# Two heads' scores issued in turn, a padded up-projection and a new order of head groups in a two-layer hybrid attention trunk

## The chip, the cores and the metric

The kernel runs on one core of a Trainium2 chip. The metric is the time of one execution on the device, in microseconds (us); of several runs the median counts. TensorE appears in the views as PE (matmuls) and PEld (loads of the stationary operand), VectorE as DVE, ScalarE as ACT, GpSimd as POOL, SyncE, whose queue issues the transfers, as SP.

## The reference, cut to what matters

Two layers over 512 tokens of width 1024. In each, one projection of the normed stream feeds five groups of four heads of width 64; their outputs go through one output projection, and a gated MLP of width 2816 with a short causal convolution follows.

```python
q_a = _heads(_rms_norm(cq, ...) @ mla_w_uq[l], 4)       # latent rank 192 -> 4 x 96
kv_a = _heads(_rms_norm(ckv, ...) @ mla_w_ukv[l], 4)    # latent rank 128
o_a = _dense_causal_attention(q_a, k_a, v_a, 96 ** -0.5)               # "mla"
o_b = _dense_causal_attention(q_b, k_b, v_b, 64 ** -0.5, decay)        # "fox"
o_c = _moba_attention(q_c, k_c, v_c, 64 ** -0.5)                       # "moba"
o_d = _diff_causal_attention(q1, q2, k1, k2, v_d, lam, 32 ** -0.5)     # "diff"
o_e = _memory_attention(q_e, k_e, v_e, 64 ** -0.5)                     # "mem", 256 keys
x = x + concat(o_a, o_b, o_c, o_d, o_e) @ w_o[l]
x = x + (silu(conv(n @ w_gate)) * (n @ w_up)) @ w_down
```

With 512 tokens every past key is within moba's choice, so that fox and moba are causal over all keys, with 128, 256, 384 and 512 keys for the four blocks of 128 rows; mem always has 256.

## The kernel before, in words

Tokens come in four blocks of 128. The heads of a group are worked on in pairs. A pair's queries and keys of width 64 lie in one tile `qk_t`: head 0 in partitions 0 to 63, head 1 in 64 to 127. Every operand of a product is held as a high and a low part in float32r, and a product is three passes: high by high, high by low, low by high. A score block of fox, moba or mem is thus three matmuls that read 64 partitions (TensorE's records say `64*128`: 64 rows and 128 columns of the array in use). Mla's heads are 96 wide; diff's are stacked to 128 rows and need one pass.

`Pair.step` (line 687) is one head and one row block: it takes one PSUM bank of the tag `s` (there are two), issues the three passes through `passes` (line 471), and then VectorE reduces the row minimum out of the bank (`soft`, line 623) and frees it, ScalarE takes the exponential (628), the rows are scaled (636, 638), TensorE transposes them (`put_pt`, 645) and they are copied into `pt_t`. `Pair.close` (754) multiplies with the values (776; for mem 768): here the two heads take turns, and they stand in different columns of the array (`128*64`). Fox adds a decay bias that POOL makes from a tile `R` per head (703, 708).

The latent up-projection (`up_proj`, 1247) multiplies plain float32 tiles: 128 rows of the latent, then its last 64, then the keys' and values' part. A float32 matmul is two records in the trace, a float32r one is one.

The order on each engine is fixed when the program is built. The work is written as tasks that ask for a buffer or for a turn on an engine at an assumed duration (`mm`, `tr`, `vec`, ... at lines 59 to 100). `Flow.run` gives out the turns by these durations: of the operations that are ready, the one that can start first, and of those the one of the earliest task. The list `ORDER` (924) sets which task is earlier: `p.` projects a pair, `a.` attends, `w.` is a group's part of the output projection, `kv.` the memory's keys and values. The chip then runs each engine's list in that order, and each instruction waits for what it needs.

Of the kernel before, what the change touches and what calls it, by code (L numbers as in the profile page):

```python
# [9 lines left out]
F32 = mybir.dt.float32  # L10
# [8 lines left out]
D = 1024  # L19
# [13 lines left out]
# 500000 ** (-i / 16) in float32, i = 0..15: the rotary frequencies of the  # L33
# 32-wide rotation; those of the 16- and 8-wide ones are every 2nd and 4th.
# [6 lines left out]
# packed small vectors, one row per layer  # L41
# [24 lines left out]

def tr(n):
    return "T", 109.0 * n
# [40 lines left out]
class Ticket(Event):  # L109
    # a place in the line for a buffer that is handed out in the order of asking  # L110
# [10 lines left out]
class Flow:  # L121
    # ns from the end of an operation to where an engine can use what it made
    LAT = {"T": dict(T=0, V=196, A=197), "V": dict(T=202, V=127, A=128, P=155, D=130),
           "A": dict(T=217, V=142, A=127, P=170), "P": dict(T=149, V=60, A=60, P=88),
           "D": dict.fromkeys("TVAPD", 2000)}

    # the engines that are short of time count for more where there is a choice
# [40 lines left out]
    def grant(self, tag):  # L168
        # first the line, then the tasks that ask without a ticket, earliest first
# [21 lines left out]
    def step(self, k, val):  # L191
        # issues what the last request was for, and takes the next one
# [81 lines left out]
def trunk(ctx: ExitStack, tc: tile.TileContext, x_in, mem, pos, norms, sm, lam, cols, conv,  # L274
# [10 lines left out]
    SLOTS = {"ws": 2, "wh": 6, "wl": 6, "qk": 4, "pt": 3, "v": 5, "kt": 1, "sk": 1, "mx": 2, "e": 5, "R": 1,  # L285
             "hr": 3, "qn": 3, "sq": 2, "st": 24, "acc": 2, "s": 2, "tp": 2, "o": 2}
# [14 lines left out]
    # ScalarE's tables: the set with both exp and ln, but for the gates the finer ln  # L301
# [26 lines left out]
    jp = const.tile([128, 128], I32, name="jp")  # L328
    P.iota(jp, pattern=[[1, 128]], base=0, channel_multiplier=-1)
# [6 lines left out]
    # the causal mask of a row block is the end of this one. It is MoBA's too: of the two  # L336
    # blocks of 256 keys that 512 tokens have, its top 3 are both, so that it sees every past key
# [3 lines left out]
    upto = const.tile([128, 128], F32, name="upto")  # L341
    V.tensor_scalar(upto, jp, 0.0, None, op0=OP.is_ge)
# [47 lines left out]
    # a block of weights as a sum of two float32r parts  # L390
# [94 lines left out]
    # half of the columns of a row block, transposed, into columns c0.. of dh + dl  # L485
# [21 lines left out]
    # sums of squares of the halves of a row block, as they come  # L507
# [1227 lines left out]
```

## Time and profile before

| what | value |
|---|---|
| runs | 1491.82, 1474.21, 1487.29 us |
| median | 1487.29 us |
| profiled execution, its span (no other time of it is given) | 1487.5 us |
| TensorE matmul busy | 1424.1 us, 96% of the span |
| VectorE, ScalarE, GpSimd busy | 757.1, 668.6, 810.6 us |
| mean granted TensorE clock | 0.977 of full speed |

The span falls into four parts: attention of the first layer to about 414 us, its MLP to 768, attention of the second layer to about 1132, its MLP to the end. A busy time of TensorE overlaps with the next matmul's, since they are pipelined; how much of the path a matmul takes is read from the distance between the starts of two rows.

### The profile page before, as it was taken

The page shows a single profiled execution, that of the slowest core. Times are in us where ns is not written, and L with a number is a line of the kernel's source. Part 1 is how long each engine was busy: PE and PEld are TensorE (multiplying, and loading weights), DVE is VectorE, ACT ScalarE, POOL GpSimd, SP SyncE. Part 2 cuts the span into 40 slices and gives each one's busy share as a digit, 9 for nine tenths or more (in the row PEclk, how much of TensorE's full clock was granted, in tenths as well). Part 3 has the DMA queues.
Part 4 walks back from the last instruction along what each step waited for, and adds up shares of the span by engine and source line. Part 5 has one row for each costly group of instructions (what it writes and reads, how often), then busy time and mean ns, then how long its engine had stood idle before and what let it go on. Part 6 is the DMA issues. An engine that isn't in the chain of part 4 may idle for free.

```text
span 1487.5 us, 20886 instructions
## 1 busy us (share of the span) xinstructions
PE 1424.1 (96%) x7304; PEld 1186.3 (80%) x7304; DVE 757.1 (51%) x2001; ACT 668.6 (45%) x1454; POOL 810.6 (54%) x793
## 2 busy tenths in 40 slices
PE   6999889999899999999999999989999999999998
PEld 5878778867798888888879788787778888888887
DVE  7977778856822311332048776887665231023311
ACT  5646546645544322433245475566544332233321
POOL 5657758642765445544466667666335443454443
PEclk9989999989999999999999899999899999999999
DMA  5211232103333223332231101210023322333223
GB/s 170 56 42 43 95 91 64 51 31 101 97 117 116 75 85 107 117 96 78 85 114 44 54 29 51 82 54 30 29 85 98 100 87 72 113 117 96 79 77 113
DMA packets 53112, 120.56 MB, mean 81 GB/s; under 512 B 6544, under 2 KB 7696, under 8 KB 53008
## 3 DMA queue, kind: packets, MB, share of 16 engines
q1 hardware_dynamic: 53008, 119.24, 25.6%
q8 instruction: 58, 0.95, 0.3%
q14 instruction: 46, 0.38, 0.1%
HBM read 117.11 MB, written 2.10 MB: 80 GB/s over the span
## 4 chain that ended last, share of the span: by engine, by line
PE 81%; DVE 10%; POOL 4%; issue 3%; ACT 1%; DMA 1%; SPq 0%; DVEq 0%; POOLq 0%; ACTq 0%
PE acc_p L471 28%; PE s_p L471 13%; PE o_p L471 8%; PE tp_p L471 8%; PE s_p L1596 4%; PE acc_p L1596 4%; PE tp_p L1596 4%; PE o_p L1596 4%; PE tp_p L645 3%; PE o_p L776 2%; DVE e_t L725 1%; POOL wl_t L414 1%; POOL st_t L481 1%; DVE qn_t L860 1%; DVE e_t L623 1%
## 5 line engine op out<-in xcount | busy, mean ns | idle before, releaser
L414 POOL TENSOR_TENSOR wl_t<-ws_t,wh_t 128x768 fp32r<-128x768 f32 (+2 forms) x280 | 451.3, 1616 | 442.1 <-ACT wh_t L412 426.5
L412 ACT ACTIVATE wh_t<-ws_t 128x768 fp32r<-128x768 f32 (+3 forms) x322 | 240.1, 749 | 443.5 <-DMA ws_t<-in_w_down_dram 81.7
L471 PE MATMUL acc_p<-wh_t,xh 128*128 128x384 f32 (+2 forms) x512 | 185.2, 362 | 1.3 <-ACT hr_t L313 0.7
L471 PE MATMUL acc_p<-wh_t,xl 128*128 128x384 f32 (+2 forms) x512 | 169.8, 332 | 0.0
L471 PE MATMUL acc_p<-wl_t,xh 128*128 128x384 f32 (+2 forms) x512 | 169.7, 331 | 0.0
L481 POOL TENSOR_TENSOR st_t<-st_t,misc 128x4 f32<-128x4 f32 (+4 forms) x96 | 110.6, 1155 | 80.1 <-DVE st_t L479 63.3
L628 ACT ACTIVATE e_t<-e_t,st_t 128x128 f32<-128x128 f32 (+3 forms) x192 | 105.2, 549 | 48.2 <-DVE st_t L623 42.8
L471 PE MATMUL acc_p<-wh_t,mx_t 128*128 128x512 f32 x320 | 119.0, 423 | 3.4 <-DVE x L905 3.3
L471 PEld LDWEIGHTS acc_p<-wh_t,xh 128*128 128x128 f32 x512 | 98.6, 193 | 7.4 <-issue 1.9
L471 PEld LDWEIGHTS acc_p<-wl_t,xh 128*128 128x128 f32 x512 | 98.6, 193 | 0.8
L471 PEld LDWEIGHTS acc_p<-wh_t,xl 128*128 128x128 f32 x512 | 97.9, 191 | 0.0
L623 DVE CUSTOM_DVE_ANT_0 e_t<-s_p,mask 128x256 f32<-128x256 f32 (+3 forms) x160 | 74.3, 471 | 26.8 <-PE s_p L471 20.0
L645 PE MATMUL tp_p<-identr,e_t 128*128 128x128 f32 x384 | 69.4, 282 | 13.9 <-DVE e_t L725 9.6
L471 PEld LDWEIGHTS acc_p<-wh_t,mx_t 128*128 128x128 f32 x320 | 62.7, 196 | 20.9 <-DVE x L905 5.2
L1535 DVE SCALAR_TENSOR_TENSOR e_t<-acc_p,convt,e_t 128x511 f32<-128x511 f32 x22 | 16.5, 750 | 123.3 <-ACT e_t L1533 123.3
L1535 DVE SCALAR_TENSOR_TENSOR e_t<-tp_p,convt,e_t 128x511 f32<-128x511 f32 x22 | 16.5, 750 | 121.2 <-ACT e_t L1533 121.2
L313 ACT ACTIVATE pt_t<-tp_p 128x256 f32<-128x256 f32 (+3 forms) x125 | 54.4, 437 | 52.4 <-PE tp_p L645 51.0
L645 PEld LDWEIGHTS tp_p<-identr,e_t 128*128 128x128 f32 x384 | 47.7, 143 | 33.1 <-issue 14.6
L471 PE MATMUL acc_p<-xh,wh_t 128*128 128x512 f32 (+1 forms) x192 | 72.0, 375 | 0.0
L471 PE MATMUL acc_p<-xl,wh_t 128*128 128x512 f32 (+1 forms) x192 | 71.7, 374 | 0.1
L471 PE MATMUL s_p<-xh,wh_t 128*128 128x512 f32 (+1 forms) x192 | 71.6, 373 | 0.0
L471 PE MATMUL acc_p<-xh,wl_t 128*128 128x512 f32 (+1 forms) x192 | 71.5, 373 | 0.0
(275 smaller groups left out, 3561.2 us busy)
## 6 DMA issues: line engine op xcount, KB each, us to landing
ws_t<-in_gu_dram SPq DMA_DIRECT2D x116, 384.0 KB, 3.0
ws_t<-in_w_down_dram SPq DMA_DIRECT2D x88, 256.0 KB, 2.5
ws_t<-in_win_pair_dram SPq DMA_DIRECT2D x48, 384.0 KB, 3.1
ws_t<-in_w_o_dram SPq DMA_DIRECT2D x40, 256.0 KB, 2.6
pt_t<-in_norms_dram SPq DMA_DIRECT2D x12, 256.0 KB, 4.0
ws_t<-in_mkv_dram SPq DMA_DIRECT2D x8, 384.0 KB, 3.0
ws_t<-in_win_mla_dram SPq DMA_DIRECT2D x8, 356.0 KB, 3.0
x<-in_x_dram SPq DMA_DIRECT2D x8, 256.0 KB, 6.9
```

Of the source, the lines that this page charges most:

```text
L313: A.activation(out, in_, AF.Copy)
L412: A.activation(self.h[:, :n], stg[:, :n], AF.Copy)
L414: ENG[e].tensor_tensor(out=self.l[:, :n], in0=stg[:, :n], in1=f32(self.h[:, :n]), op=OP.subtract)
L471: T.matmul(dst, lt, rh, start=first and i == 0, stop=last and i == n - 1)
L481: P.tensor_tensor(r[:, :n], v[:, :n], mhalf[:, :n], op=OP.pow)
L623: V.tensor_tensor_reduce(out=e[:, :n], in0=sbank[:, :n], in1=bias, scale=-scale, scalar=BIG, op0=OP.add, op1=OP.min, accum_out=st[:, 0:1])
L628: A.activation(e[:, :n], e[:, :n], AF.Exp, bias=st[:, 0:1], scale=-1.0, accum_out=st[:, 1:2])
L645: T.transpose(tp[:, j * 128:(j + 1) * 128], e[:, j * 128:(j + 1) * 128], ident)
L725: V.scalar_tensor_tensor(e[:, :n], e2[:, :n], st[:, 8:9], e[:, :n], op0=OP.mult, op1=OP.add)
L776: T.matmul(ob[h, 128 * j:512], self.src.vt[:, j, h], mv, start=j == 0, stop=j == 3)
L1535: V.scalar_tensor_tensor(c[:, 1:], bg[:, :S - 1], convt[:, f, 1:2], c[:, 1:], op0=OP.mult, op1=OP.add)
L1596: T.matmul(dbs[t][h], lt, (w.h, w.l)[wi][:, :512], start=fi == 0 and lt is gh and wi == 0, stop=fi == HALF_F - 1 and lt is gl)
```

## The change

- In fox, moba and mem one task (`scores`) now issues the score passes of both heads of a pair, head 0 and head 1 in turn, into both `s` banks; two further tasks (`rows`) do the softmax of one head each. It asks for both banks, and for both `e` buffers, before it issues anything. Mla and diff keep `step`.
- The 64 last rows of the latent are padded with zeros to 128, and so are the weights; two memsets on POOL per layer are new.
- `mm` and `tr` assume other durations, `mm2` is new: they change the order that is written, and no instruction.
- `ORDER` takes the first fox pair ahead of the second mla pair, and other places of mem, moba and `w.`.
- There are two `R` buffers. To make room, the triangle `upto` is built anew in each layer (one iota on POOL, one comparison on VectorE), the convolution's weights of 88 columns are loaded after the attention and not at the start, and `st` has 19 buffers and not 24.

```diff
 def mm(n, passes=1):
-    return "T", passes * (2 + max(107.0, 0.417 * n))
+    return "T", passes * max(109.0, 13.0 + 0.4155 * n)
...
+def mm2(n, passes):
+    return "T", passes * max(109.0, 16.0 + 0.4155 * n) + 200.0
...
 def tr(n):
-    return "T", 109.0 * n
+    return "T", 109.0 * n - 70.0
...
-            for a in range(2):
-                tk = ticket("pt")
-                op = task(self.open(a, tk))
-                heads.append([task(self.step(a, i, op)) for i in range(NT)])
+            tks = [ticket("pt") for _ in range(2)]
+            ops = [task(self.open(a, tk)) for a, tk in enumerate(tks)]
+            if kind in ("mla", "diff"):
+                for a in range(2):
+                    heads[a] = [task(self.step(a, i, ops[a])) for i in range(NT)]
+            else:
+                self.sc = [None] * NT
+                for i in range(NT):
+                    both = task(self.scores(i, ops))
+                    for a in range(2):
+                        heads[a].append(task(self.rows(a, i, both)))
...
+        def scores(self, i, ops):
+            kind, p = self.kind, self.p
+            yield ops + self.src.steps[:i + 1]
+            n, mk, qc = self.place(i)
+            qk = self.src.qk
+            yield "e", 2
+            es = [sbt([128, 512], "e") for _ in range(2)]
...
+            yield "s", 2
+            sbs = [bank("s") for _ in range(2)]
...
+            yield mm2(n, 3)
+            for j in range(3):
+                for a in range(2):
+                    lt, rh = parts[a][j]
+                    T.matmul(sbs[a][:, :n], lt, rh, start=j == 0, stop=j == 2)
...
+            yield gps1(512)
+            P.memset(Lt.t[64:128, 2, :], 0.0)
...
+            yield gps1(384)
+            P.memset(Up.q[64:128, 384:768], 0.0)
...
-                                      (lat_t[0:64, 2, ts_], uqt[0:64, q1:q1 + 192])], True, True)
+                                      (lat_t[:, 2, ts_], uqt[:, q1:q1 + 192])], True, True)
...
-    ORDER = ["p.mla0", "a.mla0", "p.fox1", "p.mla1", "a.mla1", "a.fox1", "p.fox0", "a.fox0", "p.diff0",
-             "w.fox", "kv.own", "a.diff0", "w.mla", "p.diff1", "a.diff1", "p.mem", "p.moba0", "a.mem1",
-             "a.mem0", "p.moba1", "a.moba0", "a.moba1", "w.diff", "w.mem", "w.moba", "kv.next"]
+    ORDER = ["p.mla0", "a.mla0", "p.fox0", "a.fox0", "p.mla1", "a.mla1", "p.fox1", "a.fox1", "p.diff0", "w.mla",
+             "kv.own", "a.diff0", "w.fox", "p.diff1", "a.diff1", "p.mem", "a.mem0", "p.moba0",
+             "a.mem1", "p.moba1", "a.moba0", "w.diff", "a.moba1", "w.mem", "w.moba", "kv.next"]
```

First place: TensorE in mem's attention of the first layer, before. `s_p<-kt_t,qk_t` are score passes (three are one head and one block), `acc_p<-wh_t,xh` and the like are projection passes of moba, `tp_p` are transpositions: of the normed queries and keys (`qn_t`), of softmax rows (`e_t`).

```order
L471 MATMUL s_p<-kt_t,qk_t 128x256 x3
L471 MATMUL acc_p<-wh_t,xh 128x384
L471 MATMUL acc_p<-wl_t,xh 128x384
L471 MATMUL acc_p<-wh_t,xl 128x384
L1350 MATMUL tp_p<-identr,qn_t 128x128 x2
L645 MATMUL tp_p<-identr,e_t 128x128 x2
L471 MATMUL s_p<-kt_t,qk_t 128x256 x6
```

The same place now:

```order
L745 MATMUL s_p<-kt_t,qk_t 128x256 x6
L479 MATMUL acc_p<-wh_t,xh 128x384
L479 MATMUL acc_p<-wl_t,xh 128x384
L479 MATMUL acc_p<-wh_t,xl 128x384
L479 MATMUL acc_p<-wh_t,xh 128x384
L479 MATMUL acc_p<-wl_t,xh 128x384
L479 MATMUL acc_p<-wh_t,xl 128x384
L745 MATMUL s_p<-kt_t,qk_t 128x256 x6
```

Before, score passes stand in runs of three, or of six where two blocks of one head follow each other; now every run is six passes of two heads. In the whole program 66 runs become 48.

Second place: TensorE at the end of the first mla pair, first layer, before. `acc_p<-wh_t,xh` and the like are the fox projection, the eight transpositions of `e_t` are mla's last softmax rows, `o_p<-pt_t,v_t` is mla's product with the values, `acc_p<-wh_t,pt_t` the up-projection of the second pair.

```order
L471 MATMUL acc_p<-wh_t,xh 128x384
L471 MATMUL acc_p<-wl_t,xh 128x384
L471 MATMUL acc_p<-wh_t,xl 128x384
L1350 MATMUL tp_p<-identr,qn_t 128x128 x2
L645 MATMUL tp_p<-identr,e_t 128x128 x8
L1350 MATMUL tp_p<-identr,qn_t 128x128 x2
L776 MATMUL o_p<-pt_t,v_t 64x512 x2
L776 MATMUL o_p<-pt_t,v_t 64x384 x2
L776 MATMUL o_p<-pt_t,v_t 64x256 x2
L776 MATMUL o_p<-pt_t,v_t 64x128 x2
L1350 MATMUL tp_p<-identr,qn_t 128x128 x2
L471 MATMUL acc_p<-wh_t,pt_t 128x192 x2
```

The same place now, from mla's last score passes (`s_p<-qk_t` of 512 keys) on; `tp_p<-identr,misc` are the transpositions for fox's bias:

```order
L479 MATMUL s_p<-qk_t 128x512 x6
L1411 MATMUL tp_p<-identr,qn_t 128x128 x4
L653 MATMUL tp_p<-identr,e_t 128x128 x8
L825 MATMUL o_p<-pt_t,v_t 64x512 x2
L825 MATMUL o_p<-pt_t,v_t 64x384 x2
L825 MATMUL o_p<-pt_t,v_t 64x256 x2
L825 MATMUL o_p<-pt_t,v_t 64x128 x2
L697 MATMUL tp_p<-identr,misc 128x128 x8
L479 MATMUL acc_p<-wh_t,pt_t 128x192 x2
```

No fox projection pass stands any longer between the last mla scores and the product with the values (twelve did); all of them have moved ahead of these scores. After the product, the transposition of normed fox queries that stood there is gone, and the transpositions of fox's bias and the second up-projection follow at once.

## Rows read from the trace of the kernel before

**Rows 1.** The page, part 1: busy us (share of the span) xinstructions.
```profile
PE 1424.1 (96%) x7304; PEld 1186.3 (80%) x7304; DVE 757.1 (51%) x2001; ACT 668.6 (45%) x1454; POOL 810.6 (54%) x793
```
**Rows 2.** Stretches: length, busy PE, PEld, DVE, ACT, POOL, clock, DMA share, GB/s.
```profile
40.00:80.00 40.00, 35.19 (x207) 29.57 (x206) 38.49 (x147) 25.20 (x65) 28.55 (x37) 1.00 0.19 53
103.00:158.00 55.00, 54.86 (x331) 44.36 (x331) 44.12 (x145) 35.38 (x96) 37.82 (x58) 1.00 0.09 30
283.00:310.00 27.00, 27.00 (x156) 20.45 (x153) 19.00 (x76) 16.96 (x52) 11.87 (x18) 1.00 0.07 23
322.00:365.00 43.00, 43.00 (x190) 30.82 (x190) 25.84 (x91) 24.18 (x63) 12.54 (x13) 0.84 0.22 65
414.00:768.00 354.00, 354.00 (x1630) 295.92 (x1629) 84.44 (x103) 121.01 (x180) 175.22 (x114) 1.00 0.31 98
```
**Rows 3.** Nine stretches at clock 0.50 inside the two attention parts, summed.
```profile
sum 67.40, PE 66.72 PEld 49.25 DVE 39.79 ACT 25.42 POOL 29.16; mean PE 7.41 PEld 5.47 DVE 4.42 ACT 2.82 POOL 3.24
```
**Rows 4.** Timeline, PE: one head's fox scores of 512 keys. Start us, length, instruction.
```profile
108.23 0.27 PE L645 MATMUL tp_p<-identr,e_t 128*128 128x128 f32 x1
108.44 0.96 PE L471 MATMUL s_p<-qk_t 64*128 64x512 f32 x3
109.33 0.44 PE L471 MATMUL acc_p<-wh_t,xh 128*128 128x384 f32 x1
109.61 0.34 PE L471 MATMUL acc_p<-wl_t,xh 128*128 128x384 f32 x1
```
**Rows 5.** Timeline: runs of three passes over 128, 384 and 256 keys.
```profile
103.21 0.55 PE L471 MATMUL s_p<-qk_t 64*128 64x128 f32 x3
103.69 0.44 PE L471 MATMUL acc_p<-wh_t,xh 128*128 128x384 f32 x1
...
106.54 0.79 PE L471 MATMUL s_p<-qk_t 64*128 64x384 f32 x3
107.25 0.44 PE L471 MATMUL acc_p<-wh_t,xh 128*128 128x384 f32 x1
...
288.93 0.62 PE L471 MATMUL s_p<-kt_t,qk_t 64*128 64x256 f32 x3
...
289.48 0.44 PE L471 MATMUL acc_p<-wh_t,xh 128*128 128x384 f32 x1
...
289.58 0.42 DVE L623 CUSTOM_DVE_ANT_0 e_t<-s_p,mask 128x256 f32<-128x256 f32 x1 [1.34 <-PE s_p L471]
```
**Rows 6.** Timeline, PE: a run of six passes over 256 keys.
```profile
283.68 0.97 PE L471 MATMUL s_p<-kt_t,qk_t 64*128 64x256 f32 x6
284.58 0.44 PE L471 MATMUL acc_p<-wh_t,xh 128*128 128x384 f32 x1
```
**Rows 7.** Timeline, PE: the latent queries' up-projection.
```profile
39.10 1.01 PE L471 MATMUL acc_p<-wh_t,pt_t 128*128 128x192 f32 x4
...
39.26 0.84 PE L471 MATMUL acc_p<-wh_t,pt_t 128*128 128x192 f32 x3
40.04 0.33 PE L1098 MATMUL tp_p<-identr,qn_t 128*128 128x128 f32 x1
```
**Rows 8.** Chain of waits in order of time: start us, us, what.
```profile
281.44 2.30 PE o_p L776 x16
...
436.28 5.44 PE s_p L471 x24
```
**Rows 9.** Line 623, the reduction out of the score bank: ns min/median/max.
```profile
L623 DVE CUSTOM_DVE_ANT_0 e_t<-s_p,mask x160: 273/425/694, 57.7 to 1089.7; 128x256 f32<-128x256 f32 x64, 128x128 f32<-128x128 f32 x32, 128x384 f32<-128x384 f32 x32, 128x512 f32<-128x512 f32 x32
```
**Rows 10.** Timeline, PE, end of the first mla pair.
```profile
67.38 0.95 PE L471 MATMUL s_p<-qk_t 96*128 96x512 f32 x3
...
74.78 2.91 PE L776 MATMUL o_p<-pt_t,v_t 128*64 128x512 f32 x16
80.28 0.77 PE L1350 MATMUL tp_p<-identr,qn_t 128*128 128x128 f32 x2 [2.59 <-DVE qn_t L853]
```

More of the change, by code (lines that the diff above doesn't have):

```diff
@@ L683, in open, with place @@
                 yield act(512)
-                A.activation(self.R, tp, AF.Copy, scale=-1.0)
+                A.activation(R, tp, AF.Copy, scale=-1.0)
                 free("tp")
+        def place(self, i):
+            n = M if self.kind == "mem" else 128 * (i + 1)
+            mk = mask[:, 0:M] if self.kind == "mem" else mask[:, 384 - 128 * i:512]
+            return n, mk, slice(128 * i, 128 * i + 128)
+        def scores(self, i, ops):
[5 more added lines that the diff above has]
+            es = [sbt([128, 512], "e") for _ in range(2)]
+            mks = [mk, mk]
+            if kind == "fox":
+                csb = misc[:, 96:112]
+                for a, e in enumerate(es):
+                    hd = 2 * p + a
+                    yield gps1(n)
+                    P.tensor_scalar(e[:, :n], self.R[a][:, :n], 1.0, csb[:, 4 * i + hd:4 * i + hd + 1],
+                                    op0=OP.mult, op1=OP.add)
+                    if i == NT - 1:
+                        free("R")
+                    yield gps(128)
+                    P.tensor_tensor(e[:, n - 128:n], e[:, n - 128:n], mask[:, 384:], op=OP.add)
+                    mks[a] = e[:, :n]
+            yield "s", 2
+            sbs = [bank("s") for _ in range(2)]
+            parts = []
+            for a in range(2):
+                r = slice(64 * a, 64 * a + 64)
+                if kind == "mem":
+                    kt = self.extra.kt
+                    qh, ql, kh, kl = qk[0][r, p, 0, qc], qk[0][r, p, 1, qc], kt[r, p, 0, :], kt[r, p, 1, :]
+                else:
+                    tl = qk[0]
+                    qh, ql, kh, kl = tl[r, 0, 0, qc], tl[r, 0, 1, qc], tl[r, 1, 0, 0:n], tl[r, 1, 1, 0:n]
+                parts.append([(qh, kh), (qh, kl), (ql, kh)])
+            yield mm2(n, 3)
+            for j in range(3):
+                for a in range(2):
+                    lt, rh = parts[a][j]
+                    T.matmul(sbs[a][:, :n], lt, rh, start=j == 0, stop=j == 2)
+            self.sc[i] = es, mks, sbs
@@ new lines, in rows, with turn @@
+        def rows(self, a, i, both):
+            yield both
+            n = self.place(i)[0]
+            es, mks, sbs = self.sc[i]
+            e, mk, sb_ = es[a], mks[a], sbs[a]
+            yield "st"
+            st = sbt([128, 16], "st")
+            yield from soft(e, n, sb_, mk, self.scale, st[:, 0:2], st[:, 2:3])
+            yield from scale_rows(e, n, st[:, 2:3])
+            yield from self.turn(a, i, e)
+        def turn(self, a, i, e):
+            free("st")
+            if self.kind == "mem":
+                yield from put_pt(e, 2, self.pt[a][:, i, :], 0)
+            else:
+                yield from put_pt(e, i + 1, self.pt[a], 384 * i)
@@ L747, in step @@
                 yield from scale_rows(e, n, st[:, 2:3])
-            free("st")
-            if kind == "mem":
-                yield from put_pt(e, 2, pt[:, i, :], 0)
-            else:
-                yield from put_pt(e, i + 1, pt, 384 * i)
+            yield from self.turn(a, i, e)
         def close(self, heads):
@@ L1158, in gates @@
             free("st", 3)
+            yield "sq", 2
+            yield "P", 300.0
+            jp = columns()
+            upto = sbt([128, 128], "sq")
+            yield vec1(128)
+            V.tensor_scalar(upto, jp, 0.0, None, op0=OP.is_ge)
             yield "s"
@@ L1167, in gates @@
                          lg[:, None, 4 * t:4 * t + 4].to_broadcast([128, n, 4]), start=False, stop=t == NT - 2)
+            free("sq", 2)
             csb = misc[:, 96:112]
```

63 lines of the change are left out of this document (21 added, 42 removed).

## The prediction

> **What bounds the kernel now.** I read the page first: TensorE is busy 96% of the span [rows 1], the others about half. Then the stretches [rows 2]: in the first MLP TensorE is busy 354.00 of 354.00 us, and nothing of the change lies there or in the second MLP, so all of it must show in the two attention parts, some 778 us. There the stretches differ. Around fox's scores (103 to 158 us), mem's (283 to 310) and moba's (322 to 365) TensorE is full while VectorE is at 80%, 70% and 60%: a TensorE instruction saved there shortens the path. From 40 to 80 us it is the other way round, VectorE at 38.49 of 40 and TensorE with 4.8 us idle (12%): what TensorE saves there is hidden. Last I read the clock: nine stretches of the attention parts, 67.4 us together, run at 0.50, which is 1.2 GHz of 2.4, with TensorE at work in nearly all of them [rows 3]. At full clock that work would take half as long, so they cost up to 33.7 us.
>
> Then the starts of single rows, since lengths overlap. The MLP's 24 passes of 512 columns take 5.44 us [rows 8], 0.227 us each or 0.443 ns per column. One head's three score passes over 512 keys should take 0.68 us; from their first start to the next row's start it is 0.89, and the first projection pass behind them then needs 0.28 until the next instead of 384 x 0.443 = 0.17 [rows 4]. So TensorE pays for going between 128 rows and 64: 0.21 us within the run, 0.11 behind it, and about 0.10 ahead (a transposition of 128 columns holds 0.21 us before the run). I take 0.41 us per run. That it belongs to the run and not to its passes is seen at 256 keys: three passes 0.55 [rows 5], six 0.90 [rows 6], the second three 0.35 = 3 x 256 x 0.443.
>
> **The change, part by part.**
>
> *Two heads at once.* Now a pair's six passes alternate between partitions 0 to 63 and 64 to 127. Do two halves of the array's rows work at the same time? No row shows that. The nearest row is the product with the values, where two heads stand in different columns: 2560 float32 columns as 16 records, of which one alone costs 0.16 us per 192 [rows 7] or 0.83 ns per column, so 4.3 us one after the other, take 2.30 [rows 8]: nearly both at once. Bounds: nothing, or one head's passes for free. I take the second, being nearest to that row. Free passes per pair: for 512, 384 and 256 keys 0.68, 0.51 and 0.35; for 128 keys 0.27 (0.48 less the 0.21 [rows 5]). Fox and moba have eight pairs over both layers, each 0.27 + 0.35 + 0.51 + 0.68 = 1.81: 14.5 us. Mem has four pairs with four blocks of 0.35: 5.6. Together 20.1 us, at full clock.
>
> The Trainium skill, page "TensorE: Matmul & The Clock Gate", section "Measured speedup vs the span model", gives 3.07 for four tiles of rows; taken for two that is 1.54, an estimate by which 14 us and not 20 would be saved, and the sum would end at 1461. No run shows it so far.
>
> *Fewer runs.* 66 runs become 48 in the order written: 18 x 0.41 = 7.4 us.
>
> *Padding.* The latent's second part used 64 rows. Four records of 192 columns take 0.94 us from 39.10 to 40.04 where one takes 0.16 [rows 7], 0.64 in all: 0.30 within and 0.10 behind, as above. On 128 rows the switch is gone and the columns are as many. Sixteen times 0.40 is 6.4 us; the first four lie in the stretch that VectorE bounds, so 4.8 count.
>
> *VectorE behind a faster TensorE.* Fox's stretch would shrink from 55 to about 49 us (two pairs 3.6, five runs fewer 2.1) with the same 44.1 us of VectorE, 90%; mem's from 27 to 22.6 with 19.0, 84%. At 80% TensorE lost nothing, at 96% 12%: in proportion it would lose 3.6 and 0.7 us per layer, 8.6 in all. Bounds 0 and 8.6; I take half, 4.3, since much of the idle from 40 to 80 us is the chain of norms, which does not stand in these stretches.
>
> *Both banks at once.* A pair's scores now need both `s` banks free, so both heads' reductions must be over (median 0.425 us, longest 0.694 [rows 9], and they start about 0.1 us after TensorE has gone on [rows 5]): 1.0 us as a rule, 1.5 at 512 keys. In the order written six projection passes (1.0 us) or more stand between most successive pairs. I count nothing; the upper bound is a rival below.
>
> *The order.* The assumed 512-column pass goes from 215 to 226 ns, against 227 in the trace [rows 8]; of the 63 us that TensorE is idle over the span [rows 1] some comes from rows that stand in an order made for other durations. Bounds: 12 us, a fifth of it, either way; I take a gain of 4, as the numbers come nearer to the rows. At the end of the first mla pair the 2.59 us wait for a normed fox query after the product [rows 10] goes, but the twelve fox passes (2.0 us) that covered part of the softmax between 67.38 and 74.78 are gone too: late next is that softmax, and I count zero.
>
> *The rest.* Four memsets and two iotas on POOL, two comparisons on VectorE: under half a microsecond each by the size of their operands, ahead of rows that wait for transfers or norms anyway; without that cover, 3 us together. The convolution's weights now come on SP's queue behind memory or MLP weights near the end of attention; they are needed one MLP block later, and would cost a landing of some 3 us per layer if late. Two `R` buffers let both heads' biases be made before the scores, on POOL, which has 17 of 55 us free in fox's stretch.
>
> Sum: 20.1 + 7.4 + 4.8 - 4.3 + 4 = 32 us off the profiled 1487.5, which is also the median of the runs (1487.29; nothing outside the span is given): **1455 us**.
>
> **The rivals.**
>
> *A, the halves don't overlap fully.* If the loads of the two halves come one after the other, about 0.10 us each (the 128-key passes are no shorter, 0.27 for three, though their columns would take 0.17), a pair of passes takes no less than 0.20: at 384 keys 0.42 of 0.51 is still saved, at 512 all 0.68, at 256 0.1, at 128 nothing. That is 8 x 1.2 + 16 x 0.1 = 11 instead of 20.1, 1464; if nothing overlaps at all, 1475. For it: no row shows two halves of rows at once. Against it: the columns.
>
> *B, the clock.* Half-clock stretches follow idle of TensorE, and the order moves where it idles. If half of their 67.4 us vanish, 16.9 us more are won: 1438. For it: they are few and each hangs on one gap. Against it: what causes the gaps, norms on VectorE, is left as it was.
>
> *C, VectorE bounds the attention.* Reductions, reciprocals, scalings and splits are all still there. If the stretches of fox, mem and moba do not shrink, only padding and order are left: 1487.5 - 4.8 - 4 = 1479; half of that loss gives 1466. For it: 80% before anything is saved. Against it: moba's stretch has 17 us of VectorE free, mem's 8. The Trainium skill, page "TensorEngine Tiling (Array Packing)", section "PSUM Bottleneck", states this rule: packing makes TensorE faster but not the emptying of PSUM, which can then bound. Before the change the trace does not show it: the reduction in [rows 5] sat idle 1.34 us until TensorE's scores came.
>
> *D, slower: TensorE waits for both banks at each pair.* The place is each of the 48 runs; all that TensorE has behind it waits too. The price is the wait by which the reductions' end comes after the rows that stand between. At 0.67 us per run the gain of 32 is gone; at 1.3 us, the whole turn-round plus one other VectorE instruction ahead of it, 62 us are lost and it is 1517. For it: two banks were enough for two blocks in flight before, now for one. Against it: the six or more passes between most runs.
>
> **How the numbers follow.** Forecast 0.50, with a range of its own from 1444 to 1466 (0 or 8.6 us for VectorE, the order 4 either side, the padding partly hidden). A 0.13, B 0.18, C 0.13, D 0.06. The range from 1436 to 1476 leaves out the lower third of B (0.06), the upper end of C (0.05) and D (0.06). A measurement of this kernel can tell about 2% from no change: below 1457.5 lie B and two thirds of the forecast case, 0.51; above 1517 D, 0.06; the rest, 0.43, is within.
>
> **What would show it.** In the profile after: the six passes of a pair over 512 keys take about 0.9 us from first start to next start and not 1.6, with two records starting within some 10 ns; 256 keys 0.55; no record of the up-projection says `64*128`; the fox stretch is 5 to 6 us shorter per layer with VectorE near 90%; the MLP parts stay at 354. A is shown by passes that start 0.1 us or more apart within a pair; C by TensorE idle with VectorE over 90% in these stretches; D by waits of TensorE's scores on line 623's reductions; B by the sum of the half-clock stretches. I am wrong if TensorE's idle time grows by more than 10 us, or if half-clock time grows, which takes back 0.5 us per us.

## The result, and the profile after

The change makes the kernel slightly slower: 1494.23 us (median of 20 runs, 1490.13 to 1498.33) against 1482.47 for the kernel before on the same chip (20 runs, 1474.21 to 1493.65). The ratio, taken over all these runs and not from the two medians, is 1.0066 with a 95% interval from 1.0043 to 1.0088: clear of no change, though less than 2%. Executions of the kernel before differ by up to 1.5%, the longer ones at a lower mean granted clock (beside run 1: 1474.54 us at 0.987 of full speed, 1496.29 at 0.974), so that a row from a single execution is good to some microseconds. Forecast were 1455 us and a range from 1436 to 1476. The profiled execution of the changed kernel spans 1496.5 us.

Page, part 1, of the kernel after; it answers to [rows 1]:

```profile
PE 1406.9 (94%) x7304; PEld 1164.8 (78%) x7304; DVE 779.6 (52%) x2022; ACT 667.3 (45%) x1451; POOL 812.5 (54%) x796
```

TensorE is busy 17 us less, and yet the end comes later: its idle time rises from 63 us (1487.5 less 1424.1) to 90 (1496.5 less 1406.9).

What the score passes do is what was forecast. Timeline of PE after (start, length, instruction): runs of a pair over 384, 512 and 256 keys with the row behind each, and an up-projection. They answer to [rows 4 to 7]:

```profile
106.44 0.79 PE L745 MATMUL s_p<-qk_t 64*128 64x384 f32 x6
107.17 0.44 PE L479 MATMUL acc_p<-wh_t,xh 128*128 128x384 f32 x1
...
111.97 0.96 PE L745 MATMUL s_p<-qk_t 64*128 64x512 f32 x6
112.86 0.55 PE L653 MATMUL tp_p<-identr,e_t 128*128 128x128 f32 x3
...
306.63 0.63 PE L745 MATMUL s_p<-kt_t,qk_t 64*128 64x256 f32 x6
307.19 0.44 PE L479 MATMUL acc_p<-wh_t,xh 128*128 128x384 f32 x1
...
48.44 0.82 PE L479 MATMUL acc_p<-wh_t,pt_t 128*128 128x192 f32 x4
49.10 0.59 PE L479 MATMUL acc_p<-wl_t,pt_t 128*128 128x256 f32 x2
```

Six passes of two heads take 0.89 us over 512 keys, 0.73 over 384 and 0.56 over 256, within 0.02 us of three passes of one head before (0.89, 0.71, 0.55). The up-projection's four records take 0.66 us where they took 0.94, and no record of it says `64*128`.

The surprise stands in a part that the diff does not touch. Stretch of 300 us in the middle of the first MLP (columns as in [rows 2]), first of the kernel before, then after:

```profile
450.00:750.00 300.00, 300.00 (x1325) 248.43 (x1324) 68.38 (x78) 98.17 (x144) 142.64 (x94) 1.00 0.29 94
```

```profile
450.00:750.00 300.00, 300.00 (x1298) 243.19 (x1297) 73.92 (x82) 97.05 (x142) 138.59 (x89) 1.00 0.30 91
```

TensorE is full in both, at the full clock, but gets through 1298 passes and not 1325: 0.2311 us each instead of 0.2264. From first to last matmul the two MLPs take 368.3 and 374.1 us, before 362.3 and 364.2: 16 us.

The two attention parts, first layer and second, before:

```profile
0.00:405.87 405.87, 367.57 (x2074) 304.03 (x2075) 312.32 (x943) 222.50 (x567) 245.96 (x307) 0.96 0.25 76
768.12:1119.17 351.05, 330.55 (x1842) 273.52 (x1839) 260.98 (x839) 201.87 (x526) 214.10 (x257) 0.95 0.18 53
```

and after:

```profile
0.00:412.53 412.53, 359.09 (x2080) 299.93 (x2081) 316.94 (x947) 226.02 (x571) 256.55 (x320) 0.95 0.25 75
780.80:1118.23 337.43, 308.42 (x1840) 256.62 (x1839) 273.80 (x853) 197.94 (x522) 210.36 (x255) 0.98 0.19 56
```

The second layer's attention is 13.6 us shorter, most of its half of the forecast (16); the first layer's is 6.7 us longer, although TensorE is busy 8.5 us less in it. What the attention lacks is lost in the first layer.

The first pair of mla ends later too. From the chain of waits after (start, us, what) and the stretch from 40 to 80 us:

```profile
87.85 3.31 PE o_p L825 x14
```

```profile
40.00:80.00 40.00, 33.45 (x182) 29.39 (x181) 36.24 (x148) 23.91 (x63) 27.14 (x38) 0.90 0.16 46
```

Its product with the values starts at 87.8 us and not at 74.78 [rows 10]; the up-projection ahead of it starts at 48.44 and not at 39.10 [rows 7]. In this stretch TensorE was already idle [rows 2] and now idles 6.6 us. The fox projection that now stands ahead is not the reason, as run 3 shows below.

Time at half clock fell: eleven such stretches in the attention parts, summed, against [rows 3]:

```profile
sum 58.03, PE 53.57 PEld 46.24 DVE 40.92 ACT 27.19 POOL 24.01; mean PE 4.87 PEld 4.20 DVE 3.72 ACT 2.47 POOL 2.18
```

Last, what TensorE waited for over the span (engine, tile, line waited for: us in total, times, longest). Before, four groups of it:

```profile
PE tp_p L645 <- DVE e_t L725: 9.6, 11, 2.5
...
PE tp_p L645 <- DVE st_t L631: 2.2, 2, 1.1
PE tp_p L1376 <- DVE sk_t L1368: 1.7, 2, 1.1
...
PE tp_p L491 <- DVE pt_t L502: 1.0, 3, 0.5
```

After, these four, one that had no counterpart (646) and the only two waits of products into score banks:

```profile
PE tp_p L653 <- DVE e_t L788: 7.8, 6, 2.7
PE tp_p L499 <- DVE pt_t L510: 7.7, 3, 3.2
PE tp_p L1437 <- DVE sk_t L1429: 7.6, 5, 3.5
PE tp_p L653 <- DVE st_t L639: 6.7, 6, 1.8
PE tp_p L653 <- DVE e_t L646: 5.8, 7, 1.6
...
PE s_p L479 <- DVE qk_t L595: 1.5, 1, 1.5
PE s_p L852 <- DVE st_t L631: 1.5, 1, 1.5
```

The new idle time stands ahead of transpositions that wait for VectorE's rows: the normed stream (510), a softmax row's reciprocal (639) and its scaling (646), diff's stacked queries and keys (`sk_t`). TensorE's waits for VectorE add up to 65.2 us over all groups, before to 44.7. Of the two products, 479 is an mla score that waits for its operand; 852, diff's norm, waits for the reduction out of an `s` bank. No score pass of fox, moba or mem (745) is among them.

### The profile page after: what moved, and what is told of

Same layout as the page of the kernel before. It is cut to its first block, busy times and chain, and to the rows that moved or that the text cites. A ratio compares the mean times of both kernels' runs of the same rounds, so it can differ in the third digit from the quotient of the medians.

```text
span 1496.5 us, 20889 instructions
## 1 busy us (share of the span) xinstructions
PE 1406.9 (94%) x7304; PEld 1164.8 (78%) x7304; DVE 779.6 (52%) x2022; ACT 667.3 (45%) x1451; POOL 812.5 (54%) x796
## 4 chain that ended last, share of the span: by engine, by line
PE 76%; DVE 14%; POOL 5%; issue 3%; DMA 1%; ACT 1%; SPq 0%; DVEq 0%; POOLq 0%; ACTq 0%
PE acc_p L479 24%; PE s_p L479 9%; PE tp_p L479 8%; PE o_p L479 8%; PE tp_p L1660 4%; PE acc_p L1660 4%; PE s_p L1660 4%; PE o_p L1660 4%; PE tp_p L653 3%; PE o_p L825 2%; POOL st_t L489 2%; PE s_p L745 2%; DVE e_t L631 1%; POOL wl_t L422 1%; DVE e_t L646 1%
## 5 line engine op out<-in xcount | busy, mean ns | idle before, releaser
L422 POOL TENSOR_TENSOR wl_t<-ws_t,wh_t 128x768 fp32r<-128x768 f32 (+3 forms) x279 | 455.7, 1636 | 459.4 <-ACT wh_t L420 456.5
L479 PE MATMUL acc_p<-wh_t,xh 128*128 128x384 f32 (+2 forms) x512 | 188.6, 368 | 5.0 <-ACT hr_t L318 2.8
L489 POOL TENSOR_TENSOR st_t<-st_t,misc 128x4 f32<-128x4 f32 (+4 forms) x96 | 113.6, 1186 | 82.7 <-DVE st_t L487 67.5
L422 DVE TENSOR_TENSOR wl_t<-ws_t,wh_t 128x768 fp32r<-128x768 f32 (+2 forms) x43 | 48.4, 1125 | 181.9 <-ACT wh_t L420 181.8
L479 PE MATMUL s_p<-xh,wh_t 128*128 128x512 f32 (+1 forms) x192 | 72.7, 379 | 0.0
```

The lines of the kernel that those rows point to most:

```text
L422: ENG[e].tensor_tensor(out=self.l[:, :n], in0=stg[:, :n], in1=f32(self.h[:, :n]), op=OP.subtract)
L479: T.matmul(dst, lt, rh, start=first and i == 0, stop=last and i == n - 1)
L489: P.tensor_tensor(r[:, :n], v[:, :n], mhalf[:, :n], op=OP.pow)
```

## The experiments

Theory T1: the MLP's passes are slower because the tiles lie elsewhere in SBUF. Its rival T2: they are slower by the clock or by what other engines do. Theories on the attention: the new list (T3), the assumed durations (T5), or the pairing itself, which asks for both banks (T4, the prediction's rival D), cost TensorE's idle time. Runs are numbered 1 to 16; "places" are starts of tiles in SBUF. Ratios stand to the kernel before on the same chip.

| run | kernel | median, us | ratio [95%] |
|---|---|---|---|
| 1 | after, all tiles 32 bytes further | 1497.56 | 1.0070 [1.0042, 1.0098] |
| 2 | before, all tiles 32 bytes further | 1499.33 | 1.0076 [1.0044, 1.0108] |
| 3 | 1 with the old list | 1523.82 | 1.0234 [1.0203, 1.0265] |
| 4 | 1 with the old durations | 1485.51 | 0.9988 [0.9961, 1.0015] |
| 5 | chains of passes alone | 507.98 | |
| 6 | 4 without pairing | 1503.49 | 1.0125 [1.0080, 1.0170] |
| 7 | 1 with old list and old durations | 1498.17 | 1.0076 [1.0042, 1.0110] |
| 8 | before with the new list | 1496.83 | 1.0077 [1.0039, 1.0115] |
| 9 | after, places mended | 1479.46 | 0.9972 [0.9947, 0.9997] |
| 10 | 9 with the old durations | 1462.81 | 0.9859 [0.9823, 0.9895] |
| 11 | 9, old duration of transpositions alone | 1471.14 | 0.9923 [0.9898, 0.9948] |
| 12 | 9, old duration of passes alone | 1484.92 | 0.9999 [0.9972, 1.0027] |
| 13 | 10 without pairing | 1480.59 | 0.9965 [0.9942, 0.9988] |
| 14 | 10 with the old list | 1478.80 | 0.9949 [0.9921, 0.9976] |
| 15 | 10 without padding | 1468.26 | 0.9877 [0.9840, 0.9915] |
| 16 | 10, heads one after the other in a run | 1462.67 | 0.9837 [0.9800, 0.9873] |

The intervals reach 4 to 7 us to either side, mostly by the spread of the kernel before. Runs 9 to 12 share one chip and runs 13 to 16 another, and within such a group medians are compared, which is finer.

**Runs 1 and 2, places.** Both add one unused tile behind the constants:

```diff
+    pad = const.tile([128, 8], F32, name="pad")
```

> The changed kernel with one unused tile of 32 bytes per partition behind the constants; nothing else is different, so every later tile starts 32 bytes further. Theory T1 (places in SBUF): in the changed kernel the tiles behind the constants start 32 bytes beside a multiple of 64, before they started on multiples; this makes an MLP pass of 512 columns take 0.231 us instead of 0.227, some 3,150 passes x 4.4 ns = 14 us, and the attention's passes of 384 columns 0.175 instead of 0.168, some 8 us. With the pad the pass is back at 0.227 and the time is 1471 to 1478. Rival T2 (the slower pass has another cause, such as the clock or what other engines do at the same time): the pass stays at 0.231 and the time at 1494. TensorE's idle time in the attention stays near 78 us by both.

> The kernel before with the same unused tile of 32 bytes: its tiles now start 32 bytes beside a multiple of 64. T1 (places in SBUF): the MLP's passes go from 0.227 to 0.231 us, the time rises by 14 us in the MLP and up to 8 us in the attention, to 1497 to 1505. T2 (another cause): nothing changes, 1483.

The 300 us of the first MLP in run 1 and in run 2:

```profile
450.00:750.00 300.00, 300.00 (x1287) 241.91 (x1286) 70.58 (x79) 96.05 (x141) 138.14 (x88) 1.00 0.30 91
```

```profile
450.00:750.00 300.00, 300.00 (x1300) 243.75 (x1299) 68.38 (x78) 95.88 (x141) 139.29 (x91) 1.00 0.30 92
```

Run 2 shows that places matter: 32 bytes make the kernel before 0.8% slower, with the order unchanged and the clock full, and an MLP pass goes from 0.2264 us to 0.2308; T2 falls. Run 1 shows that the rule assumed there was wrong: on multiples of 64 bytes the changed kernel's pass took 0.2331 and its time stayed at 1497.6.

**Runs 3 and 4, list and durations.** On top of run 1, the `ORDER` of before (3) or `mm` and `tr` of before (4):

```diff
-    return "T", passes * max(109.0, 13.0 + 0.4155 * n)
+    return "T", passes * (2 + max(107.0, 0.417 * n))
...
-    return "T", 109.0 * n - 70.0
+    return "T", 109.0 * n
```

> The changed kernel with the pad of 32 bytes and the list of head groups of before. T3 (the new list costs TensorE's idle time: the first mla pair closes 13 us later because fox's pair is ahead): the first product with the values comes back to about 75 us, TensorE's idle time falls from 78 us towards 55 and the time is 10 to 20 us below the padded kernel. Rival T4 (the idle time comes from the pairing itself, which asks for both banks and both row buffers at once): idle stays at 70 or more and the time is within 6 us of the padded kernel.

> The changed kernel with the pad of 32 bytes and the durations of before for matmuls and transpositions (the pair's own duration stays). T5 (the new durations, 70 ns less for each group of transpositions and 11 ns more for a pass, write a worse order): idle falls by 10 us or more and the time with it. Rival: the durations hardly matter, within 4 us of the padded kernel.

T3 fell: the old list is 26 us worse under the new durations, and T4's number (within 6 us) did not come either. Nor does the list delay the first mla pair. Its first product with the values in run 3, then in run 8, the kernel before with the new list:

```profile
85.54 4.13 PE L826 MATMUL o_p<-pt_t,v_t 128*64 128x512 f32 x16
```

```profile
74.53 2.91 PE L776 MATMUL o_p<-pt_t,v_t 128*64 128x512 f32 x16
```

It starts 9 to 14 us later than before in every version of the changed kernel, with the old list, without pairing or without padding too. So the cause lies in what all versions share and no run undid: the buffers of `R` and `st`, the triangle, the loads or the memsets. Which of them it is stays open.

T5 held for the time: the old durations give 12 us back. TensorE's idle time by the pages fell by only 4.4 us (87.4 in run 1, 83.0 in run 4), where 10 were expected.

**Run 5, the chains.** TensorE alone. The first loop, with offsets in steps of 32 bytes:

```python
for mo in MO:
    for so in SO:
        for i in range(24):
            k = i % 8
            T.matmul(b, w[:, so + 128 * k:so + 128 * k + 128], m[:, mo + 512 * k:mo + 512 * k + 512],
                     start=i == 0, stop=i == 23)
```

> A kernel that leaves the whole computation out: TensorE does 70 chains of 24 float32r passes of 512 columns, back to back, each chain with the stationary operand (128 x 128) and the moving one moved by some multiple of 32 bytes within SBUF; then runs of 64-row passes over 512, 256 and 128 columns in three patterns: two halves of the rows in turn (0 1 0 1 0 1), one after the other (0 0 0 1 1 1), and one half alone (0 0 0), each with four 128-row passes behind it. T1 (places in SBUF): the start-to-start time differs between chains, 0.227 us at some places and 0.230 to 0.240 at others, although nothing else runs; by it the rule can be read. T2 (other engines, the order or the clock make the pass slower): all 70 chains read 0.227. For the halves: if both halves work at once, 0 1 0 1 0 1 takes as long as 0 0 0, some 0.9 us at 512 columns with four passes behind; if they only gain by standing in turn, 0 0 0 1 1 1 takes 0.68 us more.

Stretches of five chains of 24 passes each (the counts take in passes still under way at the edges). The stationary operand starts 0, 32, 128, 192 and 256 bytes further than the moving one, counted from a multiple of 256:

```profile
12.71:18.16 5.45, 5.45 (x25) 4.50 (x24) 0.00 (x0) 0.00 (x0) 1.00 0.00 0
18.16:23.75 5.59, 5.59 (x25) 4.51 (x24) 0.00 (x0) 0.00 (x0) 1.00 0.00 0
34.96:40.56 5.60, 5.60 (x25) 4.50 (x24) 0.00 (x0) 0.00 (x0) 1.00 0.00 0
46.17:51.67 5.50, 5.50 (x25) 4.51 (x24) 0.00 (x0) 0.00 (x0) 1.00 0.00 0
57.27:62.72 5.45, 5.45 (x26) 4.51 (x25) 0.00 (x0) 0.00 (x0) 1.00 0.00 0
```

Over all 70 chains, ordered by that distance modulo 256, one pass takes 226.7 to 228.0 ns at 0, 228.7 to 229.3 at 192, and 232.3 to 234.3 everywhere else, wherever the pair as a whole lies. So it is the distance between the two operands that counts. In the kernel before all distances of the MLP's operands are 0. The change shortens what lies ahead of the weight tiles and behind `xh` by the second tile of the convolution's weights (352 bytes), and `st`, between `wh` and `wl`, by 5 x 64 = 320: `wh` comes to stand at 160 (512 - 352) and `wl` at 96 (768 - 672).

In the same run's timeline, runs of 64-row passes over 512 keys with four full passes behind: the two halves in turn, one after the other, and one half alone:

```profile
406.35 0.97 PE L53 MATMUL h<-m,w 64*128 64x512 f32 x6
407.25 1.20 PE L46 MATMUL b<-m,w 128*128 128x512 f32 x4
...
414.47 0.97 PE L53 MATMUL h<-m,w 64*128 64x512 f32 x6
415.37 1.20 PE L46 MATMUL b<-m,w 128*128 128x512 f32 x4
...
428.68 0.96 PE L53 MATMUL h<-m,w 64*128 64x512 f32 x3
429.57 1.20 PE L46 MATMUL b<-m,w 128*128 128x512 f32 x4
430.70 0.96 PE L53 MATMUL h<-m,w 64*128 64x512 f32 x3
```

Six passes take 0.90 us in either order and three take 0.89: the second half is free, even when its three passes are issued behind the first half's three.

**Runs 6, 7 and 8.** Run 6 lets fox, moba and mem use `step` again; run 7 has both edits of runs 3 and 4; run 8 is the kernel before with the new `ORDER` alone.

```diff
-            if kind in ("mla", "diff"):
+            if True:
...
+                else:
+                    tl, r = qk[0], slice(64 * a, 64 * a + 64)
+                    parts = tl[r, 0, 0, qc], tl[r, 0, 1, qc], tl[r, 1, 0, 0:n], tl[r, 1, 1, 0:n]
```

> The run with the durations of before (fourth run), but with fox's, moba's and mem's scores head by head again, as in the kernel before; padding, list of head groups, two R buffers and places in SBUF stay. What the pairing is worth by itself: by the prediction's terms 20 + 7 us of TensorE less 4 for VectorE, so 23 us slower than the fourth run, some 1508. Rival D (each pair waits for both banks and this eats the gain): within 6 us of the fourth run, TensorE's idle time falls by 15 us or more.

> The changed kernel with the pad, the list of head groups of before and the durations of before: of the change only pairing, padding and the small things are left, at the slower places. If list and durations act by themselves, 12 us for the durations and 26 for the list add up: 1497.6 - 12 + 26 = 1512. If each list only suits its durations, it is nearer to 1490.

> The kernel before with the new list of head groups and nothing else; its places in SBUF are those of before, so the MLP passes stay at 0.227. If the list is better by itself, it is 10 us or more below before; if it only suits the pairing, it is as before or slower.

Run 6: the pairing is worth 18 us, and TensorE's idle time in the attention is only 5 us shorter without it (65.5 us against 70.6 in run 4, from the records' starts and lengths), so rival D falls. Run 7: with the old list and old durations the changed kernel is 1 us ahead of run 2 (1499), but its places are slower: 0.2331 us a pass against 0.2308, 7 us over some 3,170 passes. At equal places about 8 us would be left, as run 14 shows. Run 8: the list alone makes the kernel before 0.8% slower. The list has no worth of its own; it suits a kernel or not. The durations were not run on the kernel before.

**Runs 9 and 10, places mended.** The order on every engine is unchanged; only starts of tiles move, until `xh`, `xl`, `wh`, `wl`, `qk`, `mx` and `pt` stand at multiples of 256:

```diff
-             "hr": 3, "qn": 3, "sq": 2, "st": 19, "acc": 2, "s": 2, "tp": 2, "o": 2}
+             "hr": 3, "qn": 3, "sq": 2, "st": 20, "acc": 2, "s": 2, "tp": 2, "o": 2}
...
+    pi32 = misc[:, 120:124].bitcast(I32)
+    smt_first = const.tile([128, SM_W], F32, name="smt0", tag="smt")
+    cv_first = const.tile([128, NF, 4], F32, name="convt0", tag="convt")
     xh = const.tile([128, KD, S], F32R, name="xh")
...
-    pi32 = const.tile([128, NT], I32, name="pi32")
...
-            Ly.smt = const.tile([128, SM_W], F32, name=f"smt{l}", tag="smt")
+            Ly.smt = const.tile([128, SM_W], F32, name=f"smt{l}", tag="smt") if l else smt_first
...
-            Cv.t = const.tile([128, NF, 4], F32, name=f"convt{l}", tag="convt")
+            Cv.t = const.tile([128, NF, 4], F32, name=f"convt{l}", tag="convt") if l else cv_first
```

> The changed kernel with every engine's order as it is, and only the places in SBUF mended: the small vectors and the convolution's weights lie ahead of xh, the positions in a free corner of misc, and st has 20 buffers, so that xh, xl, wh, wl, qk, mx and pt all start at multiples of 256 bytes. By the chains of the fifth run (0.2267 us where stationary and moving operand stand a multiple of 256 bytes apart, 0.229 to 0.234 elsewhere) the two MLPs go from 742 us back to 727 and the attention's passes of 384 columns from 0.175 to 0.168, 1024 passes of some 6 ns = 6 us: 1494 - 15 - 6 = 1473, a little below the kernel before. If the places are not the cause: 1494.

> The same places with the durations of before for matmuls and transpositions: the fourth run with its places mended. If both causes add up, 1485.5 less 21 for the MLP (748 to 727) less 6 for the attention: 1458, about what was forecast for the change (1455). If mending the places moves TensorE's idle time instead, 1470 or more.

The 300 us of the first MLP in run 9:

```profile
450.00:750.00 300.00, 300.00 (x1326) 248.47 (x1325) 71.86 (x81) 98.02 (x145) 139.99 (x91) 1.00 0.29 93
```

1326 passes again. The MLPs fall from 742.4 to 727.2 us and the time by 14.8. T1 is shown, and of run 5's rule this much: a multiple of 256 gives the fast pass. Its other steps do not carry over to the kernels. Run 1 has its weights at 192 and 128 and by the chains would beat the changed kernel with 160 and 96, but its pass takes 0.2331 us against 0.2311. In the kernels the two distances alternate, where each chain had one; that was not run alone. The 6 us expected in the attention did not come in full (749.9 to 746.5). Run 10 comes to 1462.8, 1.4% faster than before.

Where the durations' 17 us lie: the first attention part takes 410.2 us in run 9 and 389.6 in run 10 (idle 47.6 and 38.0, half clock 37.5 and 20.5), the second 336.3 and 336.9. So of 20.6 us in the first part 9.6 are idle time, and 17 us less at half clock are worth up to 8.5. The stretches at half clock of both parts, summed, in run 9 (twelve) and run 10 (eight):

```profile
sum 54.59, PE 50.27 PEld 41.67 DVE 35.78 ACT 25.92 POOL 24.06; mean PE 4.19 PEld 3.47 DVE 2.98 ACT 2.16 POOL 2.00
```

```profile
sum 34.15, PE 32.13 PEld 28.39 DVE 22.18 ACT 16.33 POOL 14.95; mean PE 4.02 PEld 3.55 DVE 2.77 ACT 2.04 POOL 1.87
```

One of the places: the fourth and the fifth group of transpositions of diff's first `sk_t` in the first layer. Timeline of PE in run 9 (in brackets the idle time and what ended it):

```profile
244.01 0.56 PE L1439 MATMUL tp_p<-identr,sk_t 128*128 128x128 f32 x4
...
245.85 0.34 PE L481 MATMUL acc_p<-wh_t,xl 128*128 128x384 f32 x1
249.64 0.63 PE L1439 MATMUL tp_p<-identr,sk_t 128*128 128x128 f32 x4 [3.46 <-DVE sk_t L1431]
```

and in run 10:

```profile
237.12 0.63 PE L1439 MATMUL tp_p<-identr,sk_t 128*128 128x128 f32 x4 [0.35 <-DVE sk_t L1431]
...
239.67 0.28 PE L481 MATMUL acc_p<-wh_t,xl 128*128 128x256 f32 x1
239.79 0.56 PE L1439 MATMUL tp_p<-identr,sk_t 128*128 128x128 f32 x4
```

In run 9 nine projection passes of 384 columns (1.6 us) stand between the two, and TensorE then waits 3.46 us for VectorE's norm; in run 10 the order puts eighteen of 256 columns there (2.2 us), and the norm is through when TensorE comes to it. From 157 to 300 us all of TensorE's waits together are 22.4 us in run 9 and 13.8 in run 10, of it 6.7 and 0.4 for `sk_t` from VectorE.

**Runs 11 and 12, one duration each.**

> The mended changed kernel with only the transpositions' duration of before (109 ns each, instead of 70 ns less per group). If it is the shorter transpositions that write the worse order, this one is at the tenth run's time, 12 us below the ninth; if it is the passes' duration, at the ninth's.

> The mended changed kernel with only the matmul passes' duration of before. If the passes' 11 ns write the worse order, 12 us below the ninth run; if the transpositions do, at the ninth's time.

Neither expectation holds alone: the old duration of transpositions gives 8.3 us, the old one of passes costs 5.5, both together give 16.6. So the two do not add up.

**Runs 13 to 16, the terms of the forecast one by one**, each undone in run 10. Runs 13 and 14 have the edits of runs 6 and 3; runs 15 and 16:

```diff
-                                      (lat_t[:, 2, ts_], uqt[:, q1:q1 + 192])], True, True)
+                                      (lat_t[0:64, 2, ts_], uqt[0:64, q1:q1 + 192])], True, True)
...
-            for j in range(3):
-                for a in range(2):
+            for a in range(2):
+                for j in range(3):
                     lt, rh = parts[a][j]
```

> The tenth run (mended places, durations of before) with fox's, moba's and mem's scores head by head. By the forecast's terms the pairing is worth 20 + 7 - 4 = 23 us: 1486; by the sixth run against the fourth, 18: 1481. Were the pairing worth nothing by itself, 1463.

> The tenth run with the list of head groups of before. At the slower places the old list cost 13 us (1498 against 1485.5). If that is the list, 1475 here; if pairing works with either list, 1463.

> The tenth run with the latent's second part on 64 rows again, in the same order on every engine. The forecast's term: 16 times 0.40 us, of which 4.8 count: 1467 to 1469. If the switch to 64 rows is hidden behind waits there, 1463.

> The tenth run with the six passes of a pair issued head 0's three first and then head 1's three. If the halves only work at once when issued in turn, each run over 512 keys takes 1.6 us instead of 0.9 and the time rises by up to 20 us, to 1480; by the chains of the fifth run (0.902 us in either order) it stays at 1463.

Against run 16, which ran on the same chip and differs from run 10 only in the order of six passes, the pairing is worth 17.9 us, the new list 16.1, the padding 5.6 (run 15's executions are spread over 8 us), and issuing in turn nothing (1462.67 against 1462.81).

## Why the prediction was wrong

The forecast was 32 us off the time; the measured ratio is 10 us on it (0.0066 x 1485). Set against the pages, the account is short: the work was saved, and idle time took it back. In us, one execution each:

| kernel | span | TensorE busy | idle |
|---|---|---|---|
| before | 1487.5 | 1424.1 | 63.4 |
| forecast | 1455 | 32 less | as before |
| after | 1496.5 | 1406.9 | 89.6 |
| run 9, places mended | 1478.0 | 1390.7 | 87.3 |
| run 10, old durations too | 1459.5 | 1380.1 | 79.4 |
| run 13, no pairing | 1477.8 | 1400.8 | 77.0 |

With its places mended the changed kernel is busy 33 us less, as forecast (up to 6 of these are 13 us less at half clock, 67.40 against 54.59). Two steps failed: that nothing happens in the MLPs, and that idle time stays, where VectorE's 4.3 us stood against the order's 4. It grew by 26 us.

In medians, the miss of 42 us splits into 14 for the places (after against run 9), 7 for the order (4 forecast, 3 lost: run 9 against 14, which undoes list and durations), and 20 by which the other parts stay behind their 28 (20.1 + 7.4 + 4.8 - 4.3; run 14 keeps 8 of them). Each is a difference of two ratios times 1485 us, and the split hangs on the order in which the parts are put in: under the new list with the old durations the same parts are worth 32 us (run 8 against 10).

**"Nothing of the change lies there or in the second MLP": wrong, 14 us** (after against run 9). I looked at which instructions change, not at where their operands come to lie. The removal of tiles, which I costed only as commands on POOL, VectorE and the queue, moved the weights against `xh` by amounts that are no multiple of 256 bytes, and each of some 3,170 MLP passes pays 4 to 5 ns. No row of the profile before shows what a place costs; the sizes in the diff could have made me ask.

**"The order: I take a gain of 4 (12 either side)": the sign is wrong, and the size within its bound by luck.** Its two parts are larger than the bound and nearly cancel: the new list gives 13 to 16 us (run 10 against 14, 16 against 14), the new durations cost 17 (run 9 against 10). The argument was that the assumed numbers come nearer to the rows. It had looked at one of two: the pass of 512 columns does come nearer (226 against 227 ns), but the group of transpositions is now assumed 70 ns shorter, 366 ns for four. After the change:

```profile
21.62 0.60 PE L499 MATMUL tp_p<-identr,pt_t 128*128 128x128 f32 x4
21.97 0.41 PE L479 MATMUL acc_p<-wh_t,xh 128*128 128x356 f32 x1
22.22 0.32 PE L479 MATMUL acc_p<-wl_t,xh 128*128 128x356 f32 x1
22.38 0.32 PE L479 MATMUL acc_p<-wh_t,xl 128*128 128x356 f32 x1
```

The group holds only 0.35 us until the next start, but the pass behind it then needs 0.25 instead of 0.16: 0.44 us together, which is what the old duration (4 x 109 = 436 ns) assumed. Run 12 shows that a truer duration is no better by itself either: with the short transpositions, the truer pass gains 5.5 us (run 9 against 12), with the old ones it costs 8.3 (11 against 10). The order is a choice among many, and single choices moved the time by up to 26 us (run 1 against 3); 12 either side was too narrow for them, and a direction could not be argued from the durations.

**Idle time "as before": wrong, 26 us more.** My own sign of being wrong, more than 10 us of it, came. By the pages the durations are 8 us of it (run 9 against 10) and the pairing 2.4 (run 10 against 13); the list alone adds 9.3 on the kernel before (72.7 in run 8). Without pairing and with the old durations 13.6 us more than before are still there (run 13): the list, or the small parts that all versions share and that I held for 3 us, the late first mla pair among their signs. How it divides between them stays open.

**The pairing in the best version** gives 17.9 us where 23 were forecast (27.5 less 4.3 for VectorE). By the pages it saves 20.7 us of work where 27.5 were counted, and costs 2.4 of idle time where 4.3 were: it falls short in saved work, not in waits.

**What was right.** Two halves of the rows do work at once: "one head's passes for free" was the right bound. The Trainium skill, page "TensorE: Matmul & The Clock Gate", section "Measured speedup vs the span model", gives 3.07 for four tiles of 32 rows; here there are two of 64 rows, and both take 0.90 us where one takes 0.89, so this case does not show a loss like that. The price of a run, 0.41 us, holds: in run 5 three passes over 512 keys take 0.89 where 3 x 0.227 = 0.68 would be bare, and from the start of the four full passes behind them to the next run it is 1.13 where 4 x 0.227 = 0.91 would be, together 0.43.

**The rivals.** D did not happen: no pair's run waits for a bank in the list of waits, and TensorE idles nearly as much without pairing (run 6). A fell: two records stand 3 to 20 ns apart within a pair. B went the forecast way but small in the changed kernel: half-clock time fell by 9 us, worth up to half of that. In run 10 it is down to 34.15 us, the half that B assumed, so that up to 17 of that run's 21 us can be the clock's; without pairing it is as low (30.74 in run 13), so the pairing's 18 us are not. C is half right: TensorE's waits for VectorE grew by 20 us (44.7 to 65.2), but ahead of transpositions that need a softmax row or a norm, not at the emptying of score banks. The Trainium skill, page "TensorEngine Tiling (Array Packing)", section "PSUM Bottleneck", names the latter; no run here shows it. A list changes much: with the old list and durations the paired kernel keeps 8 us of gain (run 14), with the new list and old durations 21.

## What to carry to other kernels

When a diff adds, removes or resizes a tile, ask where the operands of the busiest matmuls come to lie against each other before calling the untouched part untouched; a stretch in the middle of an unchanged loop, with the number of passes in it, shows it in one row. Forecast saved work and idle time apart, and compare both with the page: here the first came and the second took it back. Where the order of issue is made from a list and assumed durations, try these with the kernel that they are for; here neither could be argued. Undo each part in the best version as well as adding it to the version before: the list that cost the old kernel 11 us was worth 16 in the changed one with the old durations.

## What the runs showed of the hardware that was not expected

- In chains of passes on TensorE alone, with one distance throughout a chain, a pass of float32r over 512 columns takes 0.227 us when the stationary tile starts a multiple of 256 bytes from the moving one, 0.229 at 192, 0.232 to 0.234 elsewhere (70 chains, run 5). In the kernels, where two distances alternate, it is 0.226 with both at 0 and 0.231 to 0.233 else.
- Passes on rows 64 to 127 that are issued behind three passes on rows 0 to 63 stand beside those and not behind them. In run 5 the issue was three of the first half, then three of the second; the six recorded starts are 0, 10, 337, 346, 568 and 578 ns. The records do not name the half, but three passes of one half alone start at 0, 337 and 568, so that starts 10 ns apart belong to different halves. A whole kernel so written takes the same time (runs 10 and 16). The Trainium skill, page "TensorE: Matmul & The Clock Gate", section "The mechanism", says that matmuls start in the order in which they are issued, with no reordering; by that rule the second half's passes could not stand beside the first's here, and the measurement differs: six passes 0.90 us, three 0.89.
